# Decay factors of the recurrent heads: made for 256 tokens at a time in place of 128, on VectorE and ScalarE alone, with single buffers

## The chip, the cores and the metric

One Trainium2 chip, one core of it. The time is the device time of one launch in microseconds, here over 3 runs of the kernel before: median 1244.76 (1244.07 to 1244.89). One further execution was recorded by the profiler; all rows below are from it.

## The reference

One decoder layer on 1024 tokens of width 1024, float32:

```python
n   = rms_norm(x);  proj = n @ w_in                    # q, k, v of 4 attention heads, q, k, v, gate of 4 recurrent heads
o_diff = diff_attention(...)                           # two softmax maps per head, causal, distance penalty
o_gla  = gla_chunked(gq, gk, gv, log_alpha)            # S_t = diag(exp(g_t)) S_{t-1} + k_t^T v_t ; o_t = q_t S_t
h   = x + concat(o_diff, rms_norm(o_gla) * silu(gout)) @ w_out
out = h + (silu(m @ w_gate) * (m @ w_up)) @ w_down     # m = rms_norm(h)
```

The change touches only `gla_chunked`, the gated linear attention. Inside a chunk it needs, for tokens t >= s and the running sum b of the log gates, the sum over k of q[t,k] k[s,k] exp(b[t,k] - b[s,k]).

## The kernel before, in words

The weights and activations of the large products are split into two rounded parts each, and every product is three matrix products (`mm3`, L259 to 262). Three stages follow one another: the input projection with both kinds of heads beside it, the output projection, and the feed-forward part.

**The projection stage.** The eight column blocks of `BLOCKS` (L47) are projected in turn, each for 8 tiles of 128 tokens: 24 matrix products into one bank of PSUM (two banks, tag "mm"), then an evacuation, half on ScalarE and half on VectorE (for example `evac_a`, L532: L537 and L538). Heads work beside the projection. The four recurrent heads come in two pairs (`GlaPair`), each pair in two halves of 512 tokens, each half in four windows of 128 tokens.

**A half of a pair** runs these tasks: `gates` (Z) and `turned` (A), then `prepare` (G, L584), which makes the running sums bT (L595) and scaled copies of q and k; per window `factors` (F, L612), `intra` (I, L641) and `outputs` (O, L659), and at the end a normalization.

**factors** cuts the pairs (t, s) of a window into 7 levels: at level lv, with c = 2^lv, tokens are taken in groups of 2c; s lies in the first c of a group, t in the second, and the reference point is the last token of the first c. The X tile holds, for each level, the differences to that point (L626, L627: two subtractions of 64 columns a level; the first three levels on GpSimd, the other four on VectorE), then their exponential (L628, ScalarE, all levels at once). Q is the exponential of the second parts times q (L632, VectorE). Then X is multiplied in place by k (L637): levels 0 and 1 on GpSimd, levels 2 to 6 on VectorE. X and Q have two buffers each, so a window can be prepared while the one before it is used.

**intra** makes one matrix product for each level (`pa`, L650) into two PSUM banks, levels 0 to 3 and 4 to 6, and VectorE copies the valid places by a mask into `at` (L655). `outputs` multiplies `at` with v (`pgo`, L667), adds the state's part and updates the state.

**The order of the work.** A planner, `Order` (L85), decides at what point between the projection's products a task's instructions are written. It keeps a modelled time `now`, advanced by the products of the projection (`tick`), a credit of 0.8 of that time for other tasks, and an account of how long VectorE and ScalarE will be busy (`load`, fed by each task's `work`). A task is ready when each predecessor has ended by the given delay ago and, where that delay is above zero, when the predecessor's work is through by the account (L112 to 117). Tasks are scanned in the order in which they were added. A task is forced where a ring of buffers needs what it releases (`make_room`, L749) and at the end of the stage. Behind the planner the framework orders each engine's queue itself, with the order of writing as priority. Task F costs no TensorE time; I has 1.5, and one I0 may be written at G + 6.0 x SLACK (SLACK is 1.1) at the earliest.

Of the kernel before, what the change touches and what calls it, by code (L numbers as in the profile page):

```python
# [9 lines left out]
F32 = mybir.dt.float32  # L10
F32R = mybir.dt.float32r
I32 = mybir.dt.int32
AF = mybir.ActivationFunctionType
# [5 lines left out]
P = 128  # L19
# [9 lines left out]
NLEV = 7  # L29


PACE = 0.8
CAP = 2.0
SLACK = 1.1
# [50 lines left out]
class Order:  # L85
# [55 lines left out]
    def tick(self, cost):  # L141

        self.now += cost
        self.credit = min(self.credit + PACE * cost, CAP)
        while self.credit > 0:
# [14 lines left out]
def decoder_layer(ctx: ExitStack, tc, xt, vecs, lams, w_proj, w_up, w_gu, w_dn, out):  # L160
    nc = tc.nc
# [37 lines left out]
    def make_constants(tmp):  # L199
# [18 lines left out]
        nc.vector.tensor_mul(lp, lam4[:, 0:4:2, :], lam4[:, 1:4:2, :])  # L218
        nc.vector.reduce_sum(l2, lp, axis=AX.X)
        nc.scalar.activation(l2, l2, AF.Exp)  # L220
# [123 lines left out]
    class DiffHead:  # L344
# [24 lines left out]
        def normed(self, hf):  # L369
# [4 lines left out]
            ss = small.tile([P, 16], F32, name=f"dss{h}_{hf}", tag="ss16")  # L374
            nc.vector.reduce_sum(ss, sq.rearrange("p a (g d) -> p (a g) d", d=64), axis=AX.X)
            rs = rstd(ss, 16, 64, f"d{h}_{hf}")
# [94 lines left out]
        def tasks(self, hf):  # L471
# [11 lines left out]
            for i in range(4 * hf, 4 * hf + 4):  # L483
# [18 lines left out]
                if i % 4 == 0 and hf + h > 0:  # L502
# [3 lines left out]
                prev_o = O  # L506
            X = Task(lambda: emit_mixed(hf, h, self.om), 0.43, [(O, 4.0 * SLACK)], {"tr": (1, 0.9)}, {"wT": 1},
                     work=(0.0, 0.5))
# [8 lines left out]
    class GlaPair:  # L517
# [91 lines left out]
            nc.vector.tensor_mul(dj, s[:, :, 0:P], s[:, :, P : 2 * P])  # L609
            nc.vector.reduce_sum(self.dg, dj.rearrange("p a (h k) -> p (a h) k", k=64), axis=AX.X)  # L610

        def factors(self, hf, i):  # L612

            p = self.p


            X = gp.tile([P, NLEV, P], F32, name=f"X{p}_{hf}_{i}", tag="X", bufs=2)
            Q = gp.tile([P, NLEV, 2, 64], F32, name=f"Q{p}_{hf}_{i}", tag="Q", bufs=2)
            o = slice(P * i, P * i + P)
            v4 = lambda a, c: a.rearrange("p (n h c) -> p n h c", h=2, c=c)  # L620
            for lv in range(NLEV):
                c = 1 << lv
                xv, bv = v4(X[:, lv, :], c), v4(self.bT[:, o], c)
                ref = bv[:, :, 0, c - 1 : c].to_broadcast([P, 64 // c, c])
                eng = nc.gpsimd if lv < 3 else nc.vector
                eng.tensor_sub(xv[:, :, 0, :], ref, bv[:, :, 0, :])  # L626
                eng.tensor_sub(xv[:, :, 1, :], bv[:, :, 1, :], ref)  # L627
            nc.scalar.activation(X, X, AF.Exp)  # L628
            for lv in range(NLEV):
                c = 1 << lv  # L630
                xv = v4(X[:, lv, :], c)
                nc.vector.tensor_mul(  # L632
                    Q[:, lv].rearrange("p g (n c) -> p g n c", c=c),
                    xv[:, :, 1, :].unsqueeze(1).to_broadcast([P, 2, 64 // c, c]),
                    self.qT[:, :, o].rearrange("p g (n h c) -> p g n h c", h=2, c=c)[:, :, :, 1, :])
            for eng, lvs in ((nc.gpsimd, slice(0, 2)), (nc.vector, slice(2, NLEV))):
                eng.tensor_mul(X[:, lvs], X[:, lvs],  # L637
                               self.kT[:, o].unsqueeze(1).to_broadcast([P, lvs.stop - lvs.start, P]))
            self.XQ[i] = (X, Q)

        def intra(self, hf, i):  # L641

            p, (X, Q) = self.p, self.XQ.pop(i)
            at = gp.tile([P, 2, P], F32, name=f"at{p}_{hf}_{i}", tag="at", bufs=3)
            for hh in range(2):
                nc.scalar.mul(at[:, hh, :], ident8, self.dg[:, 2 * i + hh : 2 * i + hh + 1])
            for lvs in ((0, 1, 2, 3), (4, 5, 6)):
                pa = psum.tile([P, 4, 2, 64], F32, name=f"pa{p}_{hf}_{i}_{lvs[0]}", tag="ms")
                for k, lv in enumerate(lvs):
                    nc.tensor.matmul(pa[:, k], X[:, lv, :], Q[:, lv], start=True, stop=True)  # L650
                for k, lv in enumerate(lvs):
                    c = 1 << lv
                    ov = at.rearrange("p g (n h c) -> p g n h c", h=2, c=c)[:, :, :, 1, :]
                    mv = masks[:, lv, :].rearrange("p (n c) -> p n c", c=c).bitcast(I32)
                    nc.vector.copy_predicated(ov, mv.unsqueeze(1).to_broadcast([P, 2, 64 // c, c]),  # L655
                                              pa[:, k].rearrange("p g (n c) -> p g n c", c=c))
            self.at[hf, i] = at
# [48 lines left out]
        def tasks(self, hf):  # L706
            p = self.p
            add = order.tasks.append
            before = self if hf else pairs[p - 1] if p else None
            A = Task(lambda: self.turned(hf), 0.86, (), {"tr": (2, 1.6)}, work=(0.0, 1.4))  # L710
            G = Task(lambda: self.prepare(hf), 1.71, [(A, 0.0)], {"ms": (2, 1.6)}, {"e": 1}, (2.6, 1.5))
            Z = Task(lambda: self.gates(hf, G), 0.86, (), {"ms": (1, 3.0)}, {"e": 1}, (0.7, 1.8))
            G.preds.append((Z, 2.6 * SLACK))
            if before is not None:
                A.preds.append((before.last_intra, 0.0))
                Z.preds.append((before.last_intra, 0.0))
                G.preds.append((before.last_out, 0.0))
            add(Z)
            add(A)
            add(G)  # L720
            F, I, O = [], [], []
            for i in range(4):
                F.append(Task(lambda i=i: self.factors(hf, i), work=(3.0, 0.9)))
                I.append(Task(lambda i=i: self.intra(hf, i), 1.5, [(F[i], 4.0 * SLACK)], {"ms": (2, 1.6)},
                              work=(1.5, 0.6)))
                O.append(Task(lambda i=i: self.outputs(hf, i), 1.3, [(I[i], 2.0 * SLACK)], {"ms": (2, 0.8)},
                              work=(0.6, 0.3) if i < 3 else (4.5, 1.3)))
                F[i].preds.append((I[i - 2], 0.0) if i > 1 else (G, 0.0))
            I[0].preds.append((G, 6.0 * SLACK))
            if before is not None:  # L730
                O[0].preds.append((before.last_mixed, 0.0))
            for i in range(3):
                O[i + 1].preds.append((O[i], 1.0 * SLACK))
            for t in (F[0], F[1], I[0], F[2], I[1], O[0], F[3], I[2], O[1], I[3], O[2], O[3]):
                add(t)
            X = Task(lambda: self.mixed(hf), 0.86, [(O[3], 7.0 * SLACK)], {"tr": (2, 0.9)}, {"wT": 2},
                     (0.0, 1.0))
            add(X)
            self.last_intra, self.last_out, self.last_mixed = I[3], O[3], X
            released["stg"].append(G)  # L740
            released["gv"].append(O[3])
# [82 lines left out]
    gp = gqT = states = None  # L824
# [105 lines left out]
    for k, (o, n) in enumerate(OUT_COLS):  # L930
        b = NIN + k
        left = list(range(ND)) if k + 1 < len(OUT_COLS) else []
        for hf in range(2):
# [9 lines left out]
            for cc in range(n // P):  # L943
                c, w = o // P + cc, slice(P * cc, P * cc + P)
# [5 lines left out]
                h = hs[hf][c]  # L950
# [142 lines left out]
    for pr in range(NJ // 2):  # L1093
# [3 lines left out]
        X = [psum.tile([P, 512], F32, name=f"X{pr}_{m}", tag=("mm", "ms")[pr % 2]) for m in range(2)]  # L1097
# [292 lines left out]
```

## Time and profile before

| | |
|---|---|
| median of 3 runs | 1244.76 us |
| profiled execution | 1243.45 us |
| its span | 1241.7 us |
| TensorE busy | 1200.0 us (97%) |
| VectorE busy | 877.7 us (71%) |
| ScalarE busy | 574.3 us (46%) |
| GpSimd busy | 281.3 us (23%) |

Busy time is the time in which an engine has an instruction under way. Matrix products are pipelined: one starts before the one ahead of it has ended, so durations of a group add up to more than the stretch it fills. The same holds on VectorE for short instructions. [...]

### The profile page before, as it was taken

Reading aid. Unit: us, or ns where it says so; the run is one execution under the profiler, and the core shown is the slowest. Engines: PE = TensorE matmul, PEld = TensorE weight load, DVE = VectorE, ACT = ScalarE, POOL = GpSimd, SP = SyncE. Lnnn points to the kernel's source line nnn. Section 1 sums busy time; section 2 is a strip of 40 time slices with the busy share of each in tenths; the row PEclk is TensorE's granted clock in tenths of the full one; section 3 lists DMA queues with packets and bytes.
Section 4 is the critical chain, followed back from the end, with each engine's and each line's share of the span. In section 5 each row is a group of like instructions: output and inputs, shape, how many; then the busy total and the mean of one; then the engine's idle time right before and its main releaser. Section 6 shows DMA issues by size and latency. Waiting matters only on the chain.

```text
span 1241.7 us, 17110 instructions
## 1 busy us (share of the span) xinstructions
PE 1200.0 (97%) x6068; PEld 1009.5 (81%) x6068; DVE 877.7 (71%) x1804; ACT 574.3 (46%) x1171; POOL 281.3 (23%) x282
## 2 busy tenths in 40 slices
PE   7899998999889999999989999999999999999998
PEld 7789888889878977788768788888888888888787
DVE  6765489854888777536997576866678656667885
ACT  6656354555544666635643333333333335443432
POOL 5500414000431000000053444534345330000000
PEclk9999999999999999999999999999999999999999
DMA  6101010101100623221023231322223268753351
GB/s 214 44 22 53 8 52 18 52 26 61 39 31 20 193 78 120 86 93 69 1 102 152 69 113 74 127 100 96 103 85 127 89 250 303 257 153 93 94 178 69
DMA packets 57656, 121.41 MB, mean 98 GB/s; under 512 B 5969, under 2 KB 25570, under 8 KB 53346
## 3 DMA queue, kind: packets, MB, share of 16 engines
q1 hardware_dynamic: 57570, 120.31, 28.6%
q8 instruction: 48, 0.79, 0.3%
q14 instruction: 38, 0.31, 0.1%
HBM read 88.04 MB, written 32.24 MB: 97 GB/s over the span
## 4 chain that ended last, share of the span: by engine, by line
PE 79%; DVE 11%; ACT 3%; DMA 3%; issue 2%; POOL 1%; SPq 0%; DVEq 0%; ACTq 0%; POOLq 0%
PE X L262 6%; PE X L260 6%; PE X L261 6%; PE pp L260 5%; PE pp L262 5%; PE pp L261 5%; PE s L411 3%; PE Z L262 3%; PE Z L261 3%; PE Z L260 3%; PE po L455 2%; PE po L260 2%; PE po L262 2%; PE po L261 2%; PE V L262 2%
## 5 line engine op out<-in xcount | busy, mean ns | idle before, releaser
L260 PE MATMUL pp<-wh,nh 128*128 128x384 f32 (+1 forms) x512 | 184.1, 360 | 9.4 <-ACT wh L256 7.2
L261 PE MATMUL pp<-wl,nh 128*128 128x384 f32 (+1 forms) x512 | 176.3, 344 | 0.7 <-DVE wl L257 0.7
L262 PE MATMUL pp<-wh,nl 128*128 128x384 f32 (+1 forms) x512 | 176.5, 345 | 0.0
L260 PEld LDWEIGHTS pp<-wh,nh 128*128 128x128 f32 x512 | 97.7, 191 | 18.6 <-ACT wh L256 7.2
L261 PEld LDWEIGHTS pp<-wl,nh 128*128 128x128 f32 x512 | 97.6, 191 | 2.8 <-DVE wl L257 1.8
L262 PEld LDWEIGHTS pp<-wh,nl 128*128 128x128 f32 x512 | 97.0, 189 | 3.0 <-issue 2.4
L1036 POOL TENSOR_TENSOR S1f<-fr 128x512 f32<-128x512 f32 x20 | 27.3, 1366 | 247.9 <-DVE ndist L907 238.0
L1130 POOL TENSOR_TENSOR ac<-ac,gt 128x512 f32<-128x512 f32 x30 | 46.4, 1547 | 159.8 <-DVE ac L1115 151.9
L1127 ACT ACTIVATE gt<-gt 128x512 f32<-128x512 f32 x40 | 25.3, 633 | 112.1 <-DVE gt L1126 58.8
L424 ACT ACTIVATE e<-e,nm 128x128 f32<-128x128 f32 (+7 forms) x64 | 49.3, 772 | 33.2 <-DVE nm L416 33.1
L260 PE MATMUL po<-mh,wh 128*128 128x512 f32 x128 | 51.2, 402 | 0.0
L262 PE MATMUL po<-mh,wl 128*128 128x512 f32 x128 | 50.6, 395 | 0.0
L261 PE MATMUL po<-ml,wh 128*128 128x512 f32 x128 | 50.4, 394 | 0.0
L257 DVE SCALAR_TENSOR_TENSOR wl<-wr,vec,wh 128x384 fp32r<-128x384 f32 (+1 forms) x64 | 39.5, 644 | 13.7 <-ACT wh L256 13.6
L1036 POOL TENSOR_TENSOR S4f<-fr,S2f 128x512 f32<-128x512 f32 x20 | 34.0, 1700 | 52.8 <-DVE ucl L252 52.1
L551 POOL TENSOR_TENSOR go<-go,gs 128x1024 f32<-128x1024 f32 x4 | 10.2, 2546 | 143.5 <-ACT gs L550 143.5
L1128 DVE TENSOR_TENSOR gt<-gt,ndist 128x512 f32<-128x512 f32 x40 | 31.6, 789 | 15.7 <-ACT gt L1127 14.0
L252 DVE TENSOR_TENSOR ufl<-S3f,ufh 128x512 fp32r<-128x512 f32 x22 | 15.2, 691 | 38.7 <-ACT ufh L251 38.7
L256 ACT ACTIVATE wh<-wr,vec 128x384 fp32r<-128x384 f32 (+1 forms) x64 | 37.1, 613 | 11.4 <-DMA wr<-in_w_proj 9.7
L416 DVE CUSTOM_DVE_ANT_0 e<-s,ndist 128x512 f32<-128x512 f32 (+3 forms) x64 | 36.7, 586 | 7.9 <-PE s L411 6.2
L455 PE MATMUL po<-v,wT 128*128 128x128 f32 x288 | 39.8, 283 | 1.7 <-ACT wT L445 1.7
L650 PE MATMUL pa<-Q,X 128*128 128x128 f32 x224 | 32.2, 290 | 9.3 <-POOL X L637 9.2
(555 smaller groups left out, 3539.3 us busy)
## 6 DMA issues: line engine op xcount, KB each, us to landing
fr<-in_w_gu SPq DMA_DIRECT2D x22, 1024.0 KB, 4.8
A<-act SPq DMA_DIRECT2D x77, 256.0 KB, 3.1
wr<-in_w_proj SPq DMA_DIRECT2D x72, 192.0 KB, 2.4
act<-ac SPq DMA_DIRECT2D x11, 1024.0 KB, 3.9
B<-in_w_dn SPq DMA_DIRECT2D x44, 256.0 KB, 5.4
act<-sm SPq DMA_DIRECT2D x11, 768.0 KB, 5.3
h<-in_xt SPq DMA_DIRECT2D x16, 256.0 KB, 4.9
hd<-h SPq DMA_DIRECT2D x16, 256.0 KB, 2.0
```

The costliest lines, as they stand in the source:

```text
L256: nc.scalar.activation(hi, src, AF.Copy, scale=gain)
L257: nc.vector.scalar_tensor_tensor(lo, src, gain, hi.bitcast(F32), ALU.mult, ALU.subtract)
L260: nc.tensor.matmul(ps, ah, bh, start=first, stop=False, **k)
L261: nc.tensor.matmul(ps, ah, bl, start=False, stop=False, **k)
L262: nc.tensor.matmul(ps, al, bh, start=False, stop=last, **k)
L411: nc.tensor.matmul(ps[m][:, :n], self.qk["q", hq][a][r, P * iq : P * iq + P], self.qk["k", ch][b][r, :n], start=(j == 0), stop=(j == 2))
L416: nc.vector.tensor_tensor_reduce(e[m][:, 512 * ch : 512 * ch + n], ps[m][:, :n], ndist[:, o : o + n], scale=-slope, scalar=nm[:, m, 0:1] i ...
L424: nc.scalar.activation(e[m][:, :cols], e[m][:, :cols], AF.Exp, bias=nm[:, m, nch - 1 : nch], scale=-1.0, accum_out=l[:, m : m + 1])
L455: nc.tensor.matmul(po[:, 0:P], self.wT[i, g][:, P * k : P * k + P], self.v[g][:, k, :], start=(kb == 0), stop=(kb == i))
L650: nc.tensor.matmul(pa[:, k], X[:, lv, :], Q[:, lv], start=True, stop=True)
L1036: (eng.tensor_sub if op == "-" else eng.tensor_add)(r, a, b)
L1130: nc.gpsimd.tensor_mul(quarter(q), quarter(q), g)
```

## The change

The window of `factors` becomes 256 tokens, the half of a half. All subtractions and products go to VectorE. The exponential and the product with k are cut in two, levels 0 to 3 and 4 to 6. X and Q are twice as wide and have one buffer each. `intra` still works on 128 tokens and takes its slice of X and Q. There are two F tasks in a half, the second with I[1] as its predecessor (its tiles overwrite those that I[1] reads). F books (8.8, 1.9) us of VectorE and ScalarE in place of (3.0, 0.9), both I of a block come 8.0 x SLACK behind F in place of 4.0 x SLACK, the extra predecessor of I0 is dropped, and the order of adding changes.

```diff
+LEVELS = ((0, 1, 2, 3), (4, 5, 6))
+FACTORS = 8.0
-        def factors(self, hf, i):
+        def factors(self, hf, j):
...
-            X = gp.tile([P, NLEV, P], F32, name=f"X{p}_{hf}_{i}", tag="X", bufs=2)
-            Q = gp.tile([P, NLEV, 2, 64], F32, name=f"Q{p}_{hf}_{i}", tag="Q", bufs=2)
-            o = slice(P * i, P * i + P)
+            W2 = 2 * P
+            X = gp.tile([P, NLEV, W2], F32, name=f"X{p}_{hf}_{j}", tag="X", bufs=1)
+            Q = gp.tile([P, NLEV, 2, P], F32, name=f"Q{p}_{hf}_{j}", tag="Q", bufs=1)
+            o = slice(W2 * j, W2 * j + W2)
             v4 = lambda a, c: a.rearrange("p (n h c) -> p n h c", h=2, c=c)
-            for lv in range(NLEV):
-                c = 1 << lv
-                xv, bv = v4(X[:, lv, :], c), v4(self.bT[:, o], c)
-                ref = bv[:, :, 0, c - 1 : c].to_broadcast([P, 64 // c, c])
-                eng = nc.gpsimd if lv < 3 else nc.vector
-                eng.tensor_sub(xv[:, :, 0, :], ref, bv[:, :, 0, :])
-                eng.tensor_sub(xv[:, :, 1, :], bv[:, :, 1, :], ref)
-            nc.scalar.activation(X, X, AF.Exp)
...
-            for eng, lvs in ((nc.gpsimd, slice(0, 2)), (nc.vector, slice(2, NLEV))):
-                eng.tensor_mul(X[:, lvs], X[:, lvs],
-                               self.kT[:, o].unsqueeze(1).to_broadcast([P, lvs.stop - lvs.start, P]))
-            self.XQ[i] = (X, Q)
+            for lvs in LEVELS:
+                for lv in lvs:
+                    c = 1 << lv
+                    xv, bv = v4(X[:, lv, :], c), v4(self.bT[:, o], c)
+                    ref = bv[:, :, 0, c - 1 : c].to_broadcast([P, P // c, c])
+                    nc.vector.tensor_sub(xv[:, :, 0, :], ref, bv[:, :, 0, :])
+                    nc.vector.tensor_sub(xv[:, :, 1, :], bv[:, :, 1, :], ref)
+                r = slice(lvs[0], lvs[-1] + 1)
+                nc.scalar.activation(X[:, r], X[:, r], AF.Exp)
+            for lvs in LEVELS:
+                for lv in lvs:
+                    c = 1 << lv
+                    nc.vector.tensor_mul(
+                        Q[:, lv].rearrange("p g (n c) -> p g n c", c=c),
+                        v4(X[:, lv, :], c)[:, :, 1, :].unsqueeze(1).to_broadcast([P, 2, P // c, c]),
+                        self.qT[:, :, o].rearrange("p g (n h c) -> p g n h c", h=2, c=c)[:, :, :, 1, :])
+                r = slice(lvs[0], lvs[-1] + 1)
+                nc.vector.tensor_mul(X[:, r], X[:, r], self.kT[:, o].unsqueeze(1).to_broadcast([P, len(lvs), W2]))
+            self.XQ[j] = (X, Q)
         def intra(self, hf, i):
-            p, (X, Q) = self.p, self.XQ.pop(i)
+            p, (X, Q), ii = self.p, self.XQ[i // 2], i % 2
...
-                    nc.tensor.matmul(pa[:, k], X[:, lv, :], Q[:, lv], start=True, stop=True)
+                    nc.tensor.matmul(pa[:, k], X[:, lv, P * ii : P * ii + P], Q[:, lv, :, 64 * ii : 64 * ii + 64],
+                                     start=True, stop=True)
...
-                F.append(Task(lambda i=i: self.factors(hf, i), work=(3.0, 0.9)))
-                I.append(Task(lambda i=i: self.intra(hf, i), 1.5, [(F[i], 4.0 * SLACK)], {"ms": (2, 1.6)},
+                if i % 2 == 0:
+                    F.append(Task(lambda j=i // 2: self.factors(hf, j), work=(8.8, 1.9)))
+                    F[-1].preds.append((I[i - 1], 0.0) if i else (G, 0.0))
+                I.append(Task(lambda i=i: self.intra(hf, i), 1.5, [(F[i // 2], FACTORS * SLACK)], {"ms": (2, 1.6)},
...
-                F[i].preds.append((I[i - 2], 0.0) if i > 1 else (G, 0.0))
-            I[0].preds.append((G, 6.0 * SLACK))
...
-            for t in (F[0], F[1], I[0], F[2], I[1], O[0], F[3], I[2], O[1], I[3], O[2], O[3]):
+            for t in (F[0], I[0], I[1], F[1], O[0], O[1], I[2], I[3], O[2], O[3]):
```

## Rows read from the trace of the kernel before

**Rows 1.** The page's busy times: engine, busy us (share of span), instructions.
```profile
PE 1200.0 (97%) x6068; PEld 1009.5 (81%) x6068; DVE 877.7 (71%) x1804; ACT 574.3 (46%) x1171; POOL 281.3 (23%) x282
```

**Rows 2.** Busy us by stretch: from:to, length, PE PEld DVE ACT POOL, PEclk, DMA share, GB/s.
```profile
138.00:242.00 104.00, 95.70 (x605) 86.58 (x605) 87.57 (x287) 52.20 (x115) 30.18 (x56) 0.98 0.12 36
242.00:310.00 68.00, 67.99 (x442) 62.69 (x440) 35.10 (x94) 37.34 (x85) 4.79 (x2) 1.00 0.12 40
310.00:412.00 102.00, 93.88 (x605) 84.91 (x603) 86.49 (x284) 51.91 (x115) 30.11 (x56) 1.00 0.13 40
```

**Rows 3.** TensorE's waits, 138 to 412 us: waiter <- releaser, total us, times, longest.
```profile
PE pa L650 <- POOL X L637: 9.2, 4, 2.8
PE pp L260 <- DVE gv L538: 2.1, 4, 0.6
PE pgo L667 <- DVE at L655: 2.0, 2, 1.0
PE pgo L667 <- DVE X L627: 2.0, 2, 1.0
```

**Rows 4.** Timeline of TensorE: start, us, instruction, count, idle time ahead and releaser.
```profile
152.53 1.83 PE L650 MATMUL pa<-Q,X 128*128 128x128 f32 x14 [1.79 <-POOL X L637]
...
195.69 0.34 PE L261 MATMUL pp<-wl,nh 128*128 128x384 f32 x1
195.87 0.34 PE L262 MATMUL pp<-wh,nl 128*128 128x384 f32 x1
199.03 3.30 PE L650 MATMUL pa<-Q,X 128*128 128x128 f32 x14 [2.82 <-POOL X L637]
...
212.25 0.68 PE L667 MATMUL pgo<-gv,at 128*128 128x128 f32 x4 [1.02 <-DVE at L655]
...
371.31 1.83 PE L650 MATMUL pa<-Q,X 128*128 128x128 f32 x14 [2.83 <-POOL X L637]
```

**Rows 5.** Line 637 on GpSimd: durations min/median/max in ns, first and last start.
```profile
L637 POOL TENSOR_TENSOR X<-X,gkT x16: 773/1306/3601, 148.9 to 386.9; 128x256 f32<-128x256 f32 x16
```

**Rows 6.** Timeline of VectorE in the first half of the first pair.
```profile
142.70 0.32 DVE L627 TENSOR_TENSOR X<-bT 128x64 f32<-128x64 f32 x1
142.94 0.33 DVE L626 TENSOR_TENSOR X<-bT 128x64 f32<-128x64 f32 x1
...
147.18 0.21 DVE L626 TENSOR_TENSOR X<-bT 128x64 f32<-128x64 f32 x1
147.31 0.21 DVE L627 TENSOR_TENSOR X<-bT 128x64 f32<-128x64 f32 x1
...
149.86 0.81 DVE L637 TENSOR_TENSOR X<-X,gkT 128x640 f32<-128x640 f32 x1
150.60 1.29 DVE L632 TENSOR_TENSOR Q<-X,gqT 128x128 f32<-128x128 f32 x6
```

**Rows 7.** Timeline of VectorE in the second half of the first pair.
```profile
209.44 2.46 DVE L632 TENSOR_TENSOR Q<-X,gqT 128x128 f32<-128x128 f32 x7
...
215.48 1.49 DVE L632 TENSOR_TENSOR Q<-X,gqT 128x128 f32<-128x128 f32 x7
```

**Rows 8.** Busy us by stretch behind the wait at 196 us, columns as in rows 2.
```profile
200.00:202.00 2.00, 2.00 (x12) 2.00 (x11) 1.23 (x3) 0.33 (x2) 0.24 (x1) 0.50 0.00 0
```

**Rows 9.** Groups by line and form, VectorE, 138 to 412 us: busy us, mean ns, idle before.
```profile
L655 DVE COPY_PREDICATED at<-masks,pa 128x128 f32<-128x128 int32 x112 | 36.1, 335 | 3.8 <-PE pa L650 2.8 <-DVE X L626 0.2
L632 DVE TENSOR_TENSOR Q<-X,gqT 128x128 f32<-128x128 f32 x112 | 28.2, 316 | 0.1
...
L627 DVE TENSOR_TENSOR X<-bT 128x64 f32<-128x64 f32 x64 | 16.1, 251 | 0.0
L626 DVE TENSOR_TENSOR X<-bT 128x64 f32<-128x64 f32 x64 | 15.9, 248 | 8.1 <-ACT bT L595 4.3 <-PE pa L650 3.8
L637 DVE TENSOR_TENSOR X<-X,gkT 128x640 f32<-128x640 f32 x16 | 14.7, 918 | 0.0
```

**Rows 10.** The same view for ScalarE, 138 to 412 us.
```profile
L628 ACT ACTIVATE X<-X 128x896 f32<-128x896 f32 x16 | 15.2, 950 | 12.5 <-DVE X L627 12.5
```

More of the change, by code (lines that the diff above doesn't have):

```diff
@@ L629, in factors @@
[L629 to L635, printed above, removed]
-            for eng, lvs in ((nc.gpsimd, slice(0, 2)), (nc.vector, slice(2, NLEV))):
-                eng.tensor_mul(X[:, lvs], X[:, lvs],
-                               self.kT[:, o].unsqueeze(1).to_broadcast([P, lvs.stop - lvs.start, P]))
@@ L646, in intra @@
                 nc.scalar.mul(at[:, hh, :], ident8, self.dg[:, 2 * i + hh : 2 * i + hh + 1])
-            for lvs in ((0, 1, 2, 3), (4, 5, 6)):
+            for lvs in LEVELS:
                 pa = psum.tile([P, 4, 2, 64], F32, name=f"pa{p}_{hf}_{i}_{lvs[0]}", tag="ms")
                 for k, lv in enumerate(lvs):
-                    nc.tensor.matmul(pa[:, k], X[:, lv, :], Q[:, lv], start=True, stop=True)
+                    nc.tensor.matmul(pa[:, k], X[:, lv, P * ii : P * ii + P], Q[:, lv, :, 64 * ii : 64 * ii + 64],
+                                     start=True, stop=True)
                 for k, lv in enumerate(lvs):
```

## The prediction, on record before the changed kernel was run

> **What bounds the kernel now.** TensorE is busy for 1200.0 of 1241.7 us [rows 1], so a change on VectorE, ScalarE or GpSimd moves the time only where TensorE stands still or runs slowly. I therefore cut the span into stages by busy time [rows 2]. The decay factors are made in two stretches, 138 to 242 us (first pair of recurrent heads) and 310 to 412 us (second pair). TensorE is idle there for 104.00 - 95.70 = 8.3 us and 102.00 - 93.88 = 8.1 us, together 16.4. In the stretch between them, where projections and attention run without decay factors, it is idle for 0.01 of 68 us. So these two stretches are where something can be won: at most 16.4 us of idle time, and what a slow clock costs there.
>
> Next, who ended that idle time [rows 3]: 9.2 us lie in four waits of the level products (`pa`, L650) for GpSimd's product with k (L637), 4.0 us in four waits of the output product (`pgo`) for VectorE, 2.1 us in four waits of a projection for an evacuation (`gv`, L538). The last microsecond is spread over small ones.
>
> Then, what happens at such a place [rows 4]. In the second half of the first pair the last projection product starts at 195.87 and the level products only at 199.03, after 2.82 us idle; in the first half, at 152.53, it is 1.79 us. The second pair repeats the two, which makes the 9.2. Why GpSimd is late stands in [rows 5]: its product of 128x256 takes 0.77 us at best and 3.60 us at worst, and the worst ones are these, where VectorE issues its own products back to back.
>
> GpSimd also slows VectorE. Two differences of 64 columns start 0.24 us apart while GpSimd makes its three levels, and 0.13 us apart once it is done [rows 6]. Seven Q products take 2.46 us beside GpSimd's work and 1.49 us without it [rows 7]; the slow seven lie just ahead of a 1.02 us wait of TensorE at 212.25 [rows 4]. So I read the 4.0 us for VectorE as four times the 1.0 us by which GpSimd stretches a VectorE burst.
>
> [...]
>
> **The change, part by part.** VectorE's costs are start to start, from [rows 6]: 64 columns 0.13 us, 128 columns 0.20 us (the six Q products at 150.60: (1.29 - 0.08) / 6, where 0.08 is what the duration 0.21 has above the start to start of 0.13), 640 columns 0.74 us (149.86 to 150.60). The straight line through them is 0.067 + 0.00105 n us; it gives 0.34 for 256, 0.87 for 768 and 1.14 for 1024 columns.
>
> *VectorE.* For 256 tokens it has 14 differences of 128 columns (14 x 0.20 = 2.8), 7 Q products of 256 columns (7 x 0.34 = 2.4; bounds are the rows of 128 and 640, 0.20 and 0.74, and I take the line) and two k products (0.87 + 1.14 = 2.0): 7.2 us. Before, undisturbed, the same tokens took 16 x 0.13 + 14 x 0.20 + 2 x 0.74 = 6.4. VectorE thus takes over GpSimd's share for 0.8 us a block, 6.4 us over 8 blocks. As measured, with GpSimd beside it, the old instructions sum to 15.9 + 16.1 + 28.2 + 14.7 = 74.9 us of durations [rows 9]; the new ones (a duration is 0.08 us more than start to start) to 8 x (14 x 0.28 + 7 x 0.41 + 1.22 + 0.94) = 71.6. VectorE's load falls by some 3 us; load is not what the change costs.
>
> *ScalarE.* 16 exponentials of 896 columns at 0.95 us [rows 10] become 8 of 1024 and 8 of 768, as many columns and instructions as before: nothing. The first can run beside the last six differences.
>
> *TensorE.* The same 224 level products, their operands now slices of wider tiles (Q as two runs of 64 columns). No row shows such a read; the nearest is the contiguous one, 14 in 1.83 us [rows 4], 0.13 each, so I take zero. The bounds are half speed (0.23 each, as at 199.03), 22 us in all, to which I give only what lies above the range, and zero below, since nothing is left out of the product.
>
> *GpSimd's waits.* The 9.2 us go, and the 1.5 us of slow clock with them. What is late next at I0 is VectorE: from bT it has the 2.6 us that the planner books for `prepare`, then 7.2 us of factors: 142.6 + 9.8 = 152.4 in the first half, no earlier than GpSimd's end before (152.5); the second half has the same instructions and comes to the same place, 199. What avoids the wait is the order: I0's earliest time was G + 6.6 (6.0 x SLACK) and becomes G + 2.6 + 8.8 = 11.4 by the planner's VectorE account, so I0 is written 4.8 us of projection later. Against the 1.8 and 2.8 us of waiting that is a margin of 3.0 and 2.0 us. I take no new wait here; the bounds are 0 and the old 9.2.
>
> [...]
>
> *VectorE's stretch.* Without GpSimd the four delays of 1.0 us go: -4.0. Of the 2.1 us behind evacuations I count half, -1.0.
>
> *Single buffers.* Block 1's first difference overwrites the X that I1's last level product reads, so VectorE cannot work ahead: 7.2 us of factors, and the 14 mask copies of I0 and I1 at 0.335 - 0.07 [rows 9], 3.7 us, lie between I1 and I2. On TensorE the projections, O0 and O1 cover that, and I2 is written 8.8 us or more after block 1. But an evacuation queued behind the block holds one of the two projection banks; the other covers 24 products at 0.18 (195.69 to 195.87, [rows 4]), 4.3 us. I take 1.0 us per half, as the nearest row in which VectorE comes late (1.02, [rows 4]), +4.0 in all. The bounds are 0, as between 242 and 310 us, and 8 x (7.2 - 4.3) = 23 us, if each block holds a bank to its end. Another +1.0 is for what the new order leaves elsewhere.
>
> Sum: -9.2 - 1.5 - 4.0 - 1.0 + 4.0 + 1.0 = -10.7 us. The stages behind are bound by TensorE as well, so it isn't given back there. The profiled execution took 1243.45 us (span 1241.7), 1.3 below the median of 1244.76: 1243.45 - 10.7 = 1232.8, against the median 1234.
>
> **The rivals.** (a) *VectorE takes GpSimd's place at I0.* If the framework's own ordering moves I0 forward again, the 9.2 us stay under another name. For it: the readiness comes out alike, 152.4 against 152.5. Against: the planner's 4.8 us. Then 1.5 of clock, 4.0 and 1.0 go and 5.0 come: -1.5 us, 1243.
>
> (b) *The longer VectorE block holds up the projections*, and the kernel is slower. It decides where a block delays an evacuation by more than the 4.3 us of the other bank. At 7.2 - 4.3 = 2.9 in each of 8 blocks, 23 us come against the 15.7 that go: +7.5, 1252; with the mask copies in front (7.2 + 3.7 - 4.3 = 6.6) in the four second blocks alone, 26 - 15.7 = +11, 1255. For it: evacuations already came late beside blocks of 128 tokens, four times [rows 3]. Against it: by 0.6 us at most, though both blocks of a half were ready at once then. [...]
>
> (c) *The planner's account.* It books 8.8 us where it booked 2 x 3.0, 8 x 2.8 = 22 us more of VectorE in all. That may push attention tasks behind the projections that cover them, or happen to pack them better: -10 to +5, 1242 in the middle.
>
> **How the numbers follow.** Forecast (1228 to 1239 as its own range) 0.62, (a) 0.15, (b) 0.14, (c) 0.09. A measurement of this kernel tells about 0.2%, 2.5 us, from no change. Faster: 0.62, half of (a) and half of (c), 0.74. Same: most of the rest of these two, 0.11. Slower: (b) and a little of (c), 0.15. The range goes from all 16.4 + 1.5 us gone, 1227, to past (a) and the start of (b), 1247; outside are most of (b), slow reads of the slices, and a gain in other stages.
>
> **What would show it.** Right: no GpSimd row of factors; TensorE's idle time in the two stretches down from 16.4 to 6 us; `pa` waiting for no one; the level products of the first block 4 to 5 us later among the projections; differences at 0.28 us, Q products at 0.41; no clock of 0.5 there. Wrong: waits of `pa` for VectorE of 9 us (a); of projections for evacuations above 10 us (b); more idle time behind 412 us (c); level products above 0.13 us each.

## The result, and the profile after

The changed kernel takes 1258.78 us (median of 4 runs, 1255.87 to 1261.15), the kernel before 1244.83 beside it: a ratio of 1.0103 [1.0082, 1.0124], some 14 us slower. The prediction said 1234 and faster. The profiled execution of the changed kernel is the fastest of the four (1255.87).

First the page's busy times, then the stretches of [rows 2] with the two behind them (from:to, length, PE PEld DVE ACT POOL, PEclk, DMA share, GB/s). PE is TensorE, PEld its weight loads, DVE VectorE, ACT ScalarE, POOL GpSimd; PEclk is TensorE's granted clock as a share of full speed.

```profile
PE 1212.2 (97%) x6068; PEld 1019.7 (81%) x6068; DVE 876.9 (70%) x1732; ACT 573.9 (46%) x1170; POOL 219.9 (18%) x170
```

```profile
138.00:242.00 104.00, 97.31 (x605) 90.30 (x604) 81.14 (x232) 50.24 (x106) 0.00 (x0) 0.98 0.12 36
242.00:310.00 68.00, 65.32 (x399) 57.15 (x398) 37.61 (x102) 36.55 (x84) 4.75 (x2) 0.97 0.12 36
310.00:412.00 102.00, 97.53 (x622) 91.22 (x620) 78.55 (x229) 51.16 (x110) 0.00 (x0) 0.98 0.13 40
412.00:434.00 22.00, 21.58 (x134) 18.39 (x132) 13.44 (x42) 6.55 (x19) 0.00 (x0) 1.00 0.04 13
434.00:490.50 56.50, 51.91 (x291) 41.75 (x289) 39.93 (x123) 36.88 (x108) 0.00 (x0) 0.88 0.44 129
```

In the two stretches of the decay factors TensorE's idle time fell as the prediction wanted, though by half as much: 6.7 and 4.5 us, 11.2 in place of 16.4. But 242 to 310, which had none [rows 2], now has 2.7 us and 43 products fewer (399 for 442), and behind 434 us 4.6 us are idle at a granted clock of 0.88.

The waits of TensorE, 138 to 500 us (waiter, releaser, total us, times, longest): the level products now wait for VectorE (L643 is the product with k), though not by 9.2 us as they did for GpSimd [rows 3].

```profile
PE pa L655 <- DVE X L643: 7.6, 6, 2.4
PE s L415 <- DVE nm L420: 2.9, 4, 1.6
PE pmx L336 <- DVE gom L706: 2.5, 1, 2.5
```

Where did the time go? The last product of the input projection starts at 474.9 us before and at 490.3 after. Of these 15.4 us, 12.4 are left at the end of the span (1241.7 and 1254.1 us). So I compare stretches of equal work, from 138 us to that point, before and then after:

```profile
138.00:475.00 337.00, 318.74 (x2037) 287.15 (x2037) 253.71 (x797) 181.49 (x427) 65.09 (x114) 0.99 0.18 54
```

```profile
138.00:490.50 352.50, 333.66 (x2041) 298.81 (x2039) 250.67 (x725) 181.39 (x426) 4.75 (x2) 0.97 0.17 50
```

As many products (2037, 2041), and as much idle time: 18.3 and 18.8 us. The 15 us are *busy* time. Some 7 to 9 us of it are the clock: by the rounded column, 1 - 0.99 of 337 us is 3.4 and 1 - 0.97 of 352.5 is 10.6; added up stretch by stretch it is 12.9 against 3.8. The rest I read as products that run in short bursts, each with its whole duration, where they used to overlap a stream of projection products; no run shows that part by itself. The tile of the scores (`s`) shows the shift; before, then after (from:to, length, PE PEld DVE, PEclk, DMA share, GB/s):

```profile
242.00:310.00 68.00, 6.81 (x48) 3.75 (x48) 9.40 (x16) 1.00 0.12 40
310.00:434.00 124.00, 6.91 (x48) 3.92 (x48) 8.08 (x16) 1.00 0.24 69
434.00:490.50 56.50, 9.99 (x54) 5.86 (x54) 10.37 (x18) 0.97 0.35 107
```

```profile
242.00:310.00 68.00, 9.24 (x50) 4.87 (x50) 10.90 (x18) 0.97 0.12 36
310.00:434.00 124.00, 6.05 (x30) 3.07 (x30) 4.47 (x9) 0.99 0.11 35
434.00:490.50 56.50, 16.51 (x66) 9.52 (x66) 12.87 (x24) 0.88 0.44 129
```

Beside the second pair 30 score products ran where 48 had; the projection ran ahead in their place. In the first pair's stretch it ran ahead too. The projection's own products (`pp`) there, before and then after (PE PEld DVE ACT, then as above):

```profile
138.00:242.00 104.00, 64.48 (x319) 54.37 (x319) 4.38 (x13) 6.15 (x13) 0.98 0.12 36
```

```profile
138.00:242.00 104.00, 70.88 (x361) 63.17 (x361) 5.03 (x15) 7.05 (x15) 0.98 0.12 36
```

Nor is that the loss by itself: e2 below, 17 us faster, has 345 of them there and 30 score products beside the second pair too. Behind 434 us projection products are missing. Those of the changed kernel by stretch:

```profile
434.00:440.70 6.70, 4.93 (x24) 3.92 (x24) 0.00 (x0) 0.00 (x0) 1.00 0.02 4
440.70:476.90 36.20, 0.17 (x1) 0.00 (x0) 0.69 (x2) 0.47 (x1) 0.81 0.62 182
```

All work of the second of them:

```profile
440.70:476.90 36.20, 31.61 (x164) 23.86 (x164) 25.79 (x75) 23.52 (x62) 0.00 (x0) 0.81 0.62 182
```

For 36 us hardly a projection product starts. By the code, the evacuation of the tile just projected, and all that follows it, is written only once attention head 2's last output is (ring `v` in `make_room`), so what is left of that head runs alone, from scores to VectorE to scores. The longest such stretch in the kernel before is 7.7 us (at 436.8). Inside it the clock:

```profile
450.00:452.00 2.00, 0.59 (x1) 0.50 (x2) 2.00 (x7) 0.31 (x2) 0.00 (x0) 0.72 1.18 292
452.00:460.00 8.00, 8.00 (x31) 6.22 (x29) 4.13 (x10) 3.65 (x10) 0.00 (x0) 0.50 0.98 285
```

TensorE, after shorter waits, waits 1.6 us for VectorE up to 451.4; the clock falls within that wait (1.00 from 449 to 450 us, 0.50 from 451 to 452), and 8 us of work follow at 0.50. No wait in these 36 us is longer than 1.6 us, and the granted clock is 0.81.

A smaller copy of this lies at 263 us, TensorE's timeline:

```profile
263.18 0.72 PE L415 MATMUL s<-kh,ql 64*128 64x512 f32 x2
266.41 1.85 PE L336 MATMUL pmx<-ident,gom 128*128 128x128 f32 x8 [2.51 <-DVE gom L706]
268.20 0.47 PE L415 MATMUL s<-kh,qh 64*128 64x128 f32 x1
268.60 0.69 PE L264 MATMUL pp<-wh,nh 128*128 128x384 f32 x1
```

The first pair is late (its last output product starts at 256.9 us, in the kernel before at 237.4). By the planner's account ring `gv` forces this output, the tasks in front are run down, and TensorE meets `gom` unready: 2.5 us idle, then a slow clock again (0.50 from 267 to 269 us; the product at 268.60 takes 0.69 us where 0.34 is usual, [rows 4]). Lateness alone doesn't cost that: in e1 below this product is as late (255.9 us), and the wait for `gom` there is 0.7 us.

### The profile page after: what moved, and what is told of

Same layout as the page of the kernel before. It is cut to its first block, busy times and chain, and to the rows that moved or that the text cites. A ratio compares the mean times of both kernels' runs of the same rounds, so it can differ in the third digit from the quotient of the medians.

```text
span 1254.1 us, 16849 instructions
## 1 busy us (share of the span) xinstructions
PE 1212.2 (97%) x6068; PEld 1019.7 (81%) x6068; DVE 876.9 (70%) x1732; ACT 573.9 (46%) x1170; POOL 219.9 (18%) x170
## 4 chain that ended last, share of the span: by engine, by line
PE 81%; DVE 11%; ACT 4%; DMA 2%; issue 2%; SPq 0%; ACTq 0%; DVEq 0%
PE X L266 6%; PE X L265 6%; PE X L264 6%; PE pp L264 5%; PE pp L266 5%; PE pp L265 5%; PE s L415 3%; PE Z L265 3%; PE Z L266 3%; PE Z L264 3%; PE po L459 2%; PE V L265 2%; PE V L264 2%; PE V L266 2%; PE po L264 2%
## 5 line engine op out<-in xcount | busy, mean ns | idle before, releaser
L661 DVE COPY_PREDICATED at<-masks,pa 128x128 f32<-128x128 int32 x112 | 37.7, 337 | 11.1 <-PE pa L655 8.8
L420 DVE CUSTOM_DVE_ANT_0 e<-s,ndist 128x512 f32<-128x512 f32 (+3 forms) x64 | 36.8, 585 | 12.4 <-PE s L415 8.6
```

The lines of the kernel that those rows point to most:

```text
L420: nc.vector.tensor_tensor_reduce(e[m][:, 512 * ch : 512 * ch + n], ps[m][:, :n], ndist[:, o : o + n], scale=-slope, scalar=nm[:, m, 0:1] i ...
```

## The experiments

Ratios are to the kernel before, with 95% intervals; "booked" is VectorE's time in the planner's account per 256 tokens. "Buffers" of 1 come with the order of tasks that goes with them. In e4, e7, e8, e11 and e12 the delay between F and I is shortened as well; in e2, e13 and e14 it is that of the change.

| run | tokens | buffers | GpSimd | booked | us | ratio |
|---|---|---|---|---|---|---|
| before | 128 | 2 | yes | 6.0 | 1244.8 | |
| change | 256 | 1 | no | 8.8 | 1258.8 | 1.0103 [1.0082, 1.0124] |
| e1 | 128 | 2 | yes | 8.8 | 1244.4 | 0.9998 [0.9983, 1.0014] |
| e2 | 256 | 1 | no | 6.0 | 1241.4 | 0.9974 [0.9961, 0.9988] |
| e3 | 128 | 2 | no | 6.0 | 1244.7 | 0.9997 [0.9982, 1.0011] |
| e4 | 256 | 1 | no | 4.5 | 1238.2 | 0.9950 [0.9936, 0.9965] |
| e5 | 256 | 1 | no | 8.8, then 6.0 | 1251.3 | 1.0057 [1.0045, 1.0070] |
| e6 | 256 | 1 | no | 6.0, then 8.8 | 1252.0 | 1.0063 [1.0049, 1.0077] |
| e7 | 128 | 2 | yes | 4.5 | 1247.0 | 1.0016 [1.0007, 1.0026] |
| e8 | 256 | 1 | yes | 4.5 | 1250.3 | 1.0046 [1.0032, 1.0061] |
| e9 | 128 | 1 | no | 8.8 | 1238.9 | 0.9950 [0.9933, 0.9968] |
| e10 | 128 | 1 | no | 6.0 | 1240.4 | 0.9958 [0.9940, 0.9976] |
| e11 | 128 | 2 | no | 4.5 | 1249.4 | 1.0040 [1.0024, 1.0055] |
| e12 | 256 | 1 | no | 3.6 | 1248.3 | 1.0027 [1.0015, 1.0038] |
| e13 | 256 | 1 | no | 8.8 in two | 1237.0 | 0.9928 [0.9915, 0.9940] |
| e14 | 256 | 1 | no | 7.2 | 1240.5 | 0.9955 [0.9943, 0.9967] |
| e15 | 128 | 1 | yes | 6.0 | 1238.9 | 0.9943 [0.9931, 0.9956] |
| e16 | 128 | 2, order of e15 | yes | 6.0 | 1241.9 | 0.9972 [0.9954, 0.9989] |

### Is it the booking, or VectorE? (e1 to e4)

**e1**, the kernel before with the change's booking:

```diff
-                F.append(Task(lambda i=i: self.factors(hf, i), work=(3.0, 0.9)))
+                F.append(Task(lambda i=i: self.factors(hf, i), work=(4.4, 0.95)))
```

> The kernel before with one number of the planner changed: each factors task books 4.4 us of VectorE in place of 3.0 (the changed kernel's 8.8 for two windows). No instruction is added, removed or moved to another engine; only the places where tasks are written change: 36 tasks are left where the last tile of the projection stage forces attention head 2's output, against 22 before and 45 in the changed kernel. Theory A (the account: booked time pushes attention behind the projections that cover it): slower than before, about 12 us x (36 - 22) / (45 - 22) = 7, 1249 to 1256, with the loss between 430 and 480 us. Theory B (the longer VectorE block and the single buffers hold TensorE up): as before, 1243 to 1247.

1244.4: no change. A larger booked total alone costs nothing at 128 tokens. The loss that Theory A worked out from the number of tasks left (36, 22 and 45) did not come, so that number doesn't give the time.

**e2**, the changed kernel with less booked:

```diff
-                    F.append(Task(lambda j=i // 2: self.factors(hf, j), work=(8.8, 1.9)))
+                    F.append(Task(lambda j=i // 2: self.factors(hf, j), work=(6.0, 1.8)))
```

> The changed kernel with factors booking (6.0, 1.8) in place of (8.8, 1.9), which is what two windows booked before. The same instructions; 32 tasks are left at the force and the earlier force of the first pair's last output is gone. Theory A: most of the loss goes, 1244 to 1251. Theory B: stays at 1256 to 1261.

1241.4: 17 us come back with the same compute instructions in another order, 3 us more than Theory A allowed. What costs the time is set by the account; VectorE's longer block and the single buffers are still there.

**e3**, the kernel before with GpSimd out of `factors`, nothing else:

```diff
-                eng = nc.gpsimd if lv < 3 else nc.vector
+                eng = nc.vector
...
-            for eng, lvs in ((nc.gpsimd, slice(0, 2)), (nc.vector, slice(2, NLEV))):
+            for eng, lvs in ((nc.vector, slice(0, NLEV)),):
```

> The kernel before with all subtractions and all products with k on VectorE; windows of 128, two buffers and the planner's numbers as before, so the written order is as before. If GpSimd's lateness was what TensorE waited for, the 9.2 us of waits and the slow clock behind one go: 1232 to 1240. If VectorE only takes GpSimd's place (its load rises by 4 us in each half at 128-token windows): 1243 to 1248, with waits of pa for VectorE of 6 us and more.

1244.7: nothing gained. Its waits, 138 to 412 us, show why: VectorE has taken GpSimd's place, 8.0 us for the 9.2 of [rows 3]. That is the prediction's rival (a), at 128 tokens.

```profile
PE pa L650 <- DVE X L637: 3.5, 2, 1.8
PE pa L650 <- DVE X L627: 2.8, 2, 1.4
PE pa L650 <- DVE at L655: 1.7, 2, 0.9
```

**e4**, the changed kernel with a tight account:

```diff
-FACTORS = 8.0
+FACTORS = 5.5
...
-                    F.append(Task(lambda j=i // 2: self.factors(hf, j), work=(8.8, 1.9)))
+                    F.append(Task(lambda j=i // 2: self.factors(hf, j), work=(4.5, 1.8)))
```

> The changed kernel with factors booking (4.5, 1.8) and a delay of 5.5 x SLACK in place of 8.0 x SLACK: 26 tasks are left at the force, close to the 22 before. Theory A: the tail costs 2 us and not 12, GpSimd's waits are gone: 1238 to 1246. Theory B: 1256 or more, and more waits of pa for VectorE than in the changed kernel, since the level products are written earlier.

1238.2, faster than both kernels.

### Which of the two places, and whose gain is e4's? (e5 to e8)

**e5** and **e6** book 6.0 for one pair only (e5, shown here: the second; e6: the two values changed round):

```diff
-                    F.append(Task(lambda j=i // 2: self.factors(hf, j), work=(8.8, 1.9)))
+                    F.append(Task(lambda j=i // 2: self.factors(hf, j), work=(8.8, 1.9) if p == 0 else (6.0, 1.8)))
```

> The change, with the smaller booking of factors (6.0 us of VectorE, 1.8 of ScalarE, as in e2) for the second pair of recurrent heads only; the first pair keeps (8.8, 1.9). The planner's own account then still forces the first pair's last output early, and at the last block of the projection stage it has 36 tasks left in place of 45. Theory A, two places: if the 17 us between the changed kernel and e2 lie mainly behind the second pair (the tail of the projection stage from 434 us on, where TensorE is idle and its clock is low), this gives 1242 to 1249. If they lie mainly at the first pair's forced output (240 to 310 us), 1250 to 1257. Theory B' (the two add up): the saving here and the saving of e6 sum to 17 us. In the trace under the first reading: the last product of the projection starts at 475 to 480 us in place of 490.

> The reverse of e5: the smaller booking (6.0, 1.8) for the first pair of recurrent heads only, (8.8, 1.9) for the second. No early force of the first pair's last output is left in the planner's account; at the last block 44 tasks are left, the second pair's chain among them. If the loss lies mainly in the tail: 1251 to 1257, and the last product of the projection starts at 486 us or later. If it lies mainly at the first pair's forced output: 1242 to 1248. If the two add up, the savings of e5 and e6 sum to 17 us.

1251.3 and 1252.0: each place alone costs about 10 us above e2 (9.9 and 10.6), both together 17.4, some 3 us less than the sum; Theory B', that they add up, holds but for these 3 us. The traces agree. e5 keeps the wait at the first pair's forced output, and its clock behind 434 us is 1.00; e6 has no such wait, and 32 us at the end with 3 projection products. e5, the wait (138 to 500 us):

```profile
PE pmx L336 <- DVE gom L706: 3.0, 2, 2.5
```

e5, the last stretch:

```profile
434.00:490.50 56.50, 53.29 (x330) 42.68 (x330) 44.31 (x134) 40.02 (x115) 0.00 (x0) 1.00 0.50 147
```

e6, the projection's products, and then all work:

```profile
440.00:472.00 32.00, 0.84 (x3) 0.49 (x3) 0.60 (x2) 0.47 (x1) 0.89 0.72 205
```

```profile
440.00:472.00 32.00, 26.55 (x166) 19.94 (x164) 25.38 (x75) 23.02 (x63) 0.00 (x0) 0.89 0.72 205
```

**e7**, the kernel before with a tight account:

```diff
-                F.append(Task(lambda i=i: self.factors(hf, i), work=(3.0, 0.9)))
-                I.append(Task(lambda i=i: self.intra(hf, i), 1.5, [(F[i], 4.0 * SLACK)], {"ms": (2, 1.6)},
+                F.append(Task(lambda i=i: self.factors(hf, i), work=(2.25, 0.9)))
+                I.append(Task(lambda i=i: self.intra(hf, i), 1.5, [(F[i], 2.75 * SLACK)], {"ms": (2, 1.6)},
```

> A control for e4: the kernel before with its booking lowered in the same proportion (2.25 in place of 3.0 us of VectorE, delay 2.75 in place of 4.0 for the windows), nothing else changed. If e4's 6.6 us come from the wider windows on VectorE once the account no longer holds tasks back, this gives 1243 to 1247. If they come from the account alone, whatever the windows are, it gives 1237 to 1240.

1247.0, if anything slower: a tight account alone is not what helps.

**e8**, e4 with GpSimd's share given back:

```diff
-                    nc.vector.tensor_sub(xv[:, :, 0, :], ref, bv[:, :, 0, :])
-                    nc.vector.tensor_sub(xv[:, :, 1, :], bv[:, :, 1, :], ref)
+                    eng = nc.gpsimd if lv < 3 else nc.vector
+                    eng.tensor_sub(xv[:, :, 0, :], ref, bv[:, :, 0, :])
+                    eng.tensor_sub(xv[:, :, 1, :], bv[:, :, 1, :], ref)
...
-                r = slice(lvs[0], lvs[-1] + 1)
-                nc.vector.tensor_mul(X[:, r], X[:, r], self.kT[:, o].unsqueeze(1).to_broadcast([P, len(lvs), W2]))
+            for eng, r in ((nc.gpsimd, slice(0, 2)), (nc.vector, slice(2, 4)), (nc.vector, slice(4, 7))):
+                eng.tensor_mul(X[:, r], X[:, r], self.kT[:, o].unsqueeze(1).to_broadcast([P, r.stop - r.start, W2]))
```

> e4 (256 tokens, single buffers, booking 4.5 and 1.8, delay 5.5), but with GpSimd given back its share: the differences of levels 0 to 2 and the product with k of levels 0 and 1. If what e4 gains is the end of the waits for GpSimd, this gives 1243 to 1250, with pa waiting for GpSimd's X by 6 us or more. If e4 gains by the wider windows and the account, whichever engine makes the factors, it gives 1236 to 1240.

1250.3, 12 us slower than e4. (The edit also puts VectorE's first product with k behind all Q products, where e4 has it between them.) GpSimd's product of 128x512 takes 1.34 us at best and 4.15 at worst (ns, min/median/max), and the level products wait for it (138 to 412 us):

```profile
L644 POOL TENSOR_TENSOR X<-X,gkT x8: 1340/2895/4149, 150.1 to 395.3; 128x512 f32<-128x512 f32 x8
```

```profile
PE pa L656 <- POOL X L644: 10.2, 3, 4.7
```

At 256 tokens, with this account, taking GpSimd out is needed; at 128, with two buffers, it is worth nothing (e3).

### Total or lump, and the single buffers (e9 to e16)

**e9** is close to the change with its windows put back to 128 tokens (it keeps I0's extra predecessor, and one exponential and one product with k for all levels); against the kernel before, e3's edit and these lines:

```diff
-            X = gp.tile([P, NLEV, P], F32, name=f"X{p}_{hf}_{i}", tag="X", bufs=2)
-            Q = gp.tile([P, NLEV, 2, 64], F32, name=f"Q{p}_{hf}_{i}", tag="Q", bufs=2)
+            X = gp.tile([P, NLEV, P], F32, name=f"X{p}_{hf}_{i}", tag="X", bufs=1)
+            Q = gp.tile([P, NLEV, 2, 64], F32, name=f"Q{p}_{hf}_{i}", tag="Q", bufs=1)
...
-                F.append(Task(lambda i=i: self.factors(hf, i), work=(3.0, 0.9)))
+                F.append(Task(lambda i=i: self.factors(hf, i), work=(4.4, 0.95)))
...
-                F[i].preds.append((I[i - 2], 0.0) if i > 1 else (G, 0.0))
+                F[i].preds.append((I[i - 1], 0.0) if i > 0 else (G, 0.0))
...
-            for t in (F[0], F[1], I[0], F[2], I[1], O[0], F[3], I[2], O[1], I[3], O[2], O[3]):
+            for t in (F[0], I[0], F[1], I[1], O[0], F[2], I[2], O[1], F[3], I[3], O[2], O[3]):
```

> The change with its windows put back to 128 tokens and nothing else: factors on VectorE and ScalarE alone, single buffers of X and Q (the factors of a window come behind the use of the one before), and the same VectorE time booked in all, 4.4 us per 128 tokens for 8.8 per 256. Theory A1: it is the booked total that pushes tasks behind the projections that cover them; then this loses as the change does, 1253 to 1262. Theory A2: it is the lump, a block of 256 tokens for which the account lets nothing follow until all 8.8 us are through; then this gives 1243 to 1249. The planner's own account leaves 32 tasks at the last block here, 45 in the changed kernel, which speaks for A2.

1238.9, 6 us faster than before where the change is 14 slower, with the same total booked. Theory A1, the total, is out. A2, the lump, is favoured, though its range lay 4 us higher; e13 tests it on the changed kernel itself.

**e10** is e9 with `work=(3.0, 0.9)` as before.

> e3 (128 tokens, GpSimd out of the factors, booked as before) with single buffers of X and Q in place of two. It measures the term that the prediction put at +4.0 us with bounds of 0 and 23. If a single buffer holds up VectorE or TensorE: 1247 to 1256. If what lies beside it covers it: within 2 us of e3's 1244.7.

1240.4, outside both: at 128 tokens single buffers with their order don't cost 4.0 us but bring 4.

**e11** is e3 with e7's lines, **e12** is e4 with

```diff
-FACTORS = 5.5
+FACTORS = 4.5
...
-                    F.append(Task(lambda j=i // 2: self.factors(hf, j), work=(4.5, 1.8)))
+                    F.append(Task(lambda j=i // 2: self.factors(hf, j), work=(3.6, 1.8)))
```

> e3 (128 tokens, two buffers, GpSimd out of the factors) with the booking and the delay of e7 (2.25 and 2.75), which stand to the kernel before as e4's do to the changed one. It asks whether the window of 256 tokens has a part in e4's 6.6 us. If not, and GpSimd's absence together with a tight account is all of it: 1236 to 1240. If the wide window has a part: 1242 to 1246.

> The changed kernel with the account lowered once more: 3.6 us booked for factors, a delay of 4.5 for the windows (e4: 4.5 and 5.5). The planner's account leaves 25 tasks at the last block where e4 leaves 26, so what was pushed behind the projections is back already: 1237 to 1240, as e4. If the tasks are now written before VectorE can have their data, pa waits for X by more than e4's 4.4 us and the time rises to 1241 to 1246.

1249.4 and 1248.3, both slower than either branch foresaw. The account can be too tight as well. e12's waits, 138 to 412 us; in e4 the two are 4.4 and 1.7:

```profile
PE pa L655 <- DVE X L643: 7.9, 6, 2.0
PE pgq L578 <- ACT gstg L541: 6.2, 4, 2.3
```

**e13**, the changed kernel with the lump in two and the total kept:

```diff
-                    F.append(Task(lambda j=i // 2: self.factors(hf, j), work=(8.8, 1.9)))
+                    F.append(Task(lambda j=i // 2: self.factors(hf, j), work=(4.4, 0.95)))
...
-                              work=(1.5, 0.6)))
+                              work=(5.9, 1.55) if i % 2 == 0 else (1.5, 0.6)))
```

> The changed kernel with the same 8.8 us booked for a block, but half of it with factors and half with the block's first intra, so that the account lets that intra follow after half. The delay of 8.8 us behind factors stays. If the lump decides: 1238 to 1245, and the last projection product starts at 474 to 479 us. If the booked total decides, as in the changed kernel: 1254 to 1262.

1237.0, the fastest of all and 1 us below the range of the lump: 21.8 us faster than the change by that edit. Its stretches of the decay factors, to set beside [rows 2]: 3.8 and 3.0 us idle, at a clock of 1.00.

```profile
138.00:242.00 104.00, 100.17 (x644) 92.39 (x644) 86.70 (x254) 52.21 (x116) 0.00 (x0) 1.00 0.12 36
...
310.00:412.00 102.00, 98.97 (x635) 91.32 (x634) 83.84 (x249) 48.93 (x110) 0.00 (x0) 1.00 0.13 42
```

It too has a stretch without projection products at the end (20.5 us from 436.7), at a clock of 1.00; the length of that stretch alone doesn't fix the time. Nor does its clock: e9, 6 us faster than the kernel before, runs there at 0.73.

```profile
425.00:450.00 25.00, 24.43 (x107) 17.60 (x106) 18.19 (x56) 14.46 (x31) 0.00 (x0) 0.73 0.82 241
```

**e14** is the changed kernel with `work=(7.2, 1.9)`.

> The changed kernel with 7.2 us booked in place of 8.8 (the true time of a block's factors on VectorE by the prediction's count), 1.9 for ScalarE as it was. If the loss grows with the booking in proportion, from 1241.4 at 6.0 to 1258.8 at 8.8: 1249. If it is a step in the order of the work (the first pair's last output forced or not): 1240 to 1244, since the planner's account forces nothing early here and leaves 32 tasks at the last block, as at 6.0.

1240.5: a step between 7.2 and 8.8, no slope. A lump of 7.2 costs nothing.

**e15** is the kernel before with e9's lines but for the booking, GpSimd kept; **e16** is e15 with `bufs=2` again.

> The kernel before with single buffers of X and Q and the order of tasks that goes with them, GpSimd keeping its part, booked 3.0 as before. e10 is the same without GpSimd, 1240.4. If single buffers alone bring e10's gain: 1239 to 1242. If taking GpSimd out is needed for it: 1244 to 1252, with pa waiting for GpSimd's X.

> e15 with two buffers of X and Q again: the kernel before, with the order of adding of e15 (a window's factors added and allowed behind the intra of the window before) and nothing else. If the order brings e15's gain: 1237 to 1241, and pa waits for GpSimd's X by about 7 us as in e15. If one buffer is needed for it: 1243 to 1247.

1238.9 and 1241.9. GpSimd's product with k, in e15 and then in e16 (ns, min/median/max; [rows 5] before):

```profile
L637 POOL TENSOR_TENSOR X<-X,gkT x16: 853/970/1462, 149.1 to 396.9; 128x256 f32<-128x256 f32 x16
```

```profile
L637 POOL TENSOR_TENSOR X<-X,gkT x16: 737/850/1596, 149.7 to 389.3; 128x256 f32<-128x256 f32 x16
```

The 3.60 us instructions are gone though GpSimd does all it did: by the edit, the next window's factors are written only behind the `intra` of this one. With one shape, the order of the tasks alone moves the worst case from 3.60 to 1.60 us (e16); what makes GpSimd slow in the old order is not shown.

TensorE's waits did not all go. In e15 it still waits for GpSimd, in nine short waits where there were four long ones [rows 3]; in e16 that wait nearly goes, against its forecast of 7 us, and one of `pgo` for the masked copies comes. The lines of e15, then of e16, 138 to 412 us:

```profile
PE pa L650 <- POOL X L637: 7.3, 9, 1.7
```

```profile
PE pgo L667 <- DVE at L655: 7.8, 7, 1.4
PE pa L650 <- POOL X L637: 1.3, 5, 0.3
```

The order brings about half of e15's gain; since the intervals touch (0.9954 and 0.9956), how much the single buffer adds is not settled.

## Why the prediction was wrong

**The step that failed** is "The stages behind are bound by TensorE as well, so it isn't given back there", with the term it left to rival (c), outside the sum: "-10 to +5, 1242 in the middle", chance 0.09. Its sign came (from 412 us to the last projection product 5.0 us are idle, in the kernel before 1.8), at over three times its upper bound. The booking of 8.8 in one lump costs 17 us against 6.0 (e2), 18 against 7.2, the prediction's estimate (e14), 22 against the same 8.8 in two (e13). I counted the booked total (22 us more), which e1 and e9 show to be harmless. Shown is that 8.8 booked at one time costs these 22 us and 8.8 booked in two parts doesn't, with the same instructions (e13); e9 agrees.

How it acts is argued. By the code, whatever books VectorE behind a lump is through only when the lump is, and its followers wait (L112 to 117), attention's too; meanwhile the projection, which waits for nobody, is used up. The projection products that ran ahead (361 for 319) and the scores held back (30 for 48) fit that. The counts don't settle it, though: they are much the same in e2 (345 and 30). What differs more is how late the pairs end. The last output products of the two start at 256.9 and 433.3 us in the change, at 244.2 and 417.4 in e2, 246.4 and 417.7 in e14, 248.0 and 412.0 in e13. But in e5 the second pair ends at 429.7 without a slow clock behind it (1.00 from 434 to 490.5 us), and in e1 the first at 255.9 without the long wait, so lateness alone is not the price. Which of the waits in the account carries it stays open.

The other steps:

- *VectorE's prices* were right. Forecast 0.28, 0.41, 1.22 and 0.94 us; measured, VectorE's groups, 138 to 427 us:

```profile
L638 DVE TENSOR_TENSOR Q<-X,gqT 128x256 f32<-128x256 f32 x56 | 20.3, 417 | 0.8 <-ACT X L634 0.8
L631 DVE TENSOR_TENSOR X<-bT 128x128 f32<-128x128 f32 x56 | 15.9, 285 | 2.3 <-ACT bT L599 2.1
L632 DVE TENSOR_TENSOR X<-bT 128x128 f32<-128x128 f32 x56 | 15.9, 283 | 0.0
L643 DVE TENSOR_TENSOR X<-X,gkT 128x1024 f32<-128x1024 f32 x8 | 9.7, 1217 | 0.0
...
L643 DVE TENSOR_TENSOR X<-X,gkT 128x768 f32<-128x768 f32 x8 | 7.6, 945 | 0.0
```

- *Slices cost TensorE nothing*: right. The 224 level products have a mean duration of 282 ns, in the kernel before 290.
- *-9.2 for GpSimd's waits, no new wait*: mostly wrong. 7.6 us of waits for VectorE came, so 1.6 net; this is rival (a) for the most part, which kept all 9.2. The 4.8 us by which the account was to put I0 later were no margin: the first level products stand behind 544 projection products, in the kernel before behind 556, and in the second half, where they do come later (760 against 694), they wait 2.4 us all the same. e4 (4.4) and e13 (3.7) keep part of it.
- *-1.5 for the clock* (14 level products in 3.30 us and in 1.83 [rows 4], the clock at 0.50 [rows 8]): wrong. No run shows the term by itself; what came instead is a granted clock of 0.66 over 5 us in each stretch of the decay factors, behind waits for VectorE (2.43 us up to 209.57, 2.10 us up to 391.64) in place of GpSimd:

```profile
211.00:216.00 5.00, 4.57 (x21) 4.43 (x22) 3.79 (x9) 1.57 (x3) 0.00 (x0) 0.66 0.00 2
...
392.00:397.00 5.00, 5.00 (x23) 4.81 (x22) 4.95 (x16) 0.94 (x4) 0.00 (x0) 0.66 0.40 118
```

- *-4.0 for VectorE's stretch, -1.0 for evacuations*: right. The waits of `pgo` fell from 4.0 to 0.4 us (to 0.7 in e3, where GpSimd alone is gone); those of a projection for `gv` are gone.
- *+4.0 for single buffers*, and rival (b), an evacuation held behind the block: wrong in sign. No projection product waits for an evacuation up to 440 us, and at 128 tokens single buffers with their order gain (e10, e15). At 256 tokens no run has two.

Together the two stretches lost 5 us of idle time where I had 10. So the local sum was half right, and a gain of 3 us (e2) was overrun by 17 us of order. With the account split (e13) the gain is 9.0 us, near the forecast of 10.7, but that is in part luck: the waits it was made of are not all gone there (3.7 us of `pa` for VectorE), and e15 gets 7.1 us with neither wide windows nor a GpSimd freed of its part. So the gain isn't shown to be theirs.

Open: what tips between 7.2 and 8.8, by which waits of the account, and how e13 pays for its last 20 us. Two buffers at 256 tokens and a third buffer for `gv` were not tried.

## What to carry to other kernels

When an edit changes a number by which a planner orders work, price it as a change of its own: the same instructions ran in 1237 to 1259 us by how one booked cost was sized and split, and such a number is best tried at three values. Compare stretches of equal work, not idle time: here 15 us were lost without 1 us more of idle. Before an engine is relieved, see whether another order of the work is enough: with the next window's factors written behind the use of this one's (e16), GpSimd's slowest product with k went from 3.60 to 1.60 us and the kernel gained 3 us, although other waits came.

## What the runs showed of the hardware

TensorE's granted clock fell with little idle time ahead: in the changed kernel it went from 1.00 (449 to 450 us) to 0.50 (451 to 452) within a wait of 1.6 us that ended at 451.4 us, behind waits of 0.2 and 0.7, and 8 us at 0.50 followed; in the kernel before it stayed at 1.00 from 368 to 380 us, across a gap of 2.83 us at 371 us [rows 4]. And one GpSimd instruction of fixed shape, the product with k of 128x256, took 0.77 to 3.60 us [rows 5] and, with nothing changed but the order of the tasks, 0.74 to 1.60 (e16).
